# Seven-product mixers: one low half by an adding transfer, inner tiles loaded earlier in the program, weight operands placed by product width

## The chip, the cores and the metric

The kernel runs on one core of one Trainium2 chip. A core has five engines with their own instruction streams: TensorE (PE, matrix products; its weight loads are shown as PEld), VectorE (DVE), ScalarE (ACT), GpSimd (POOL) and SyncE (SP). POOL and SP serve here mainly to issue transfers (DMA). The metric is the device time of one execution in microseconds; lower is better.

## The reference

The model is a two-layer streaming encoder over 512 tokens of width 1024, all in float32. Layer 0 has an RWKV-7 mixer (12 heads of 64) beside a 4-head attention to 256 memory tokens; layer 1 has chunked attention against a shared K/V, again beside memory attention. Each layer ends with the part that the change is about, a convolutional gated mixer:

```python
def conv_glu(h, w_in, conv_w, conv_b, w_out):
    gate, val = jnp.split(h @ w_in, 2, axis=-1)          # 512 x 2816 each
    gp = jnp.pad(gate, ((0, 0), (CONV_W - 1, 0), (0, 0)))
    conv = conv_b + sum(conv_w[j] * gp[:, j:j + seq] for j in range(CONV_W))
    return (jax.nn.gelu(conv, approximate=False) * val) @ w_out
...
x = x + conv_glu(rms_norm(x, ln2[layer]), ffn_in[layer], ffn_conv[layer],
                 ffn_conv_b[layer], ffn_out[layer])
```

`w_in` is 1024 x 5632, that is 22 tiles of 128 gate columns and 22 of 128 value columns. The result must agree with float32 arithmetic, which is why the kernel splits every operand in two.

## The kernel before

**Split operands.** Every dense product runs in TensorE's fp32r format on a high part and a low part of each operand. For one weight tile W and one activation tile X there are three matmuls: Whi·Xhi, Whi·Xlo and Wlo·Xhi. The high part of a weight tile is a rounding copy (ACT). The low part is W - Whi, either a DVE subtraction, or an *adding transfer*: ACT writes -round(W) into the low tile, and then a POOL-issued DMA adds W to it from DRAM.

**Weight buffers.** Pool `wp` holds weight tiles of 128 partitions x 1024 floats (4096 bytes per partition): three for high parts (`whi`), three for low parts (`wlo`), and two (`wraw`) that hold raw weights in most stages and, under the name `wlv`, a low part in the mixers. Activations stand in long-lived tiles of 16384 bytes per partition: `r1h`/`r1l`, `r2h`/`r2l`, `th`/`tl`. Pools lay tiles out in the order of their first use, each rounded up to 32 bytes. In the program before, `r1h` and `r1l` start 32 bytes past a multiple of 128 (`cst` 2840 bytes and `vec` 1264 bytes stand ahead of them), while all `wp` tiles, `r2h`, `r2l`, `th`, `tl` and `sl` start on a multiple of 128.

**Stages.** Up to about 350 us layer 0's RWKV mixer (recurrence work woven with dense projections); to 393 us the output projection; 393 to 713 us the first conv mixer; to 925 us layer 1's attention; to 958 us the output projection; to the end the second conv mixer. In the first conv mixer the activations are U = `r2` and T = `th`/`tl`; in the second U = `r1` and T = `th`/`tl`.

**The input side of a conv mixer** (`ffn`, class `Seven`). 21 of the 22 tiles are done "by seven": the 2 x 2 block product (gate and value block against two halves of the inner dimension, two token halves of 256) takes 7 half-size products in place of 8. One *frame* does one tile j; a product (`prod`, L408) is 4 inner blocks x 3 matmuls of 256 columns, L414 for the two that use a high weight and L416 for the one that uses a low weight. A frame's seven products in order, with their weights and activations: (1) G1 against U, (2) S2 against T, (3) S3 and (4) S1 against T, (5) V2 against T, (6) G2 and (7) S4 against U. G1, V1, G2, V2 are the four raw quarter blocks of 512 columns, S1 to S4 are sums that DVE forms. Each frame also prepares the next tile's weights. The order on DVE and ACT in this stage is the program's (`keep` pins it). What a frame j issues:

- SP: `load` of tile j+1, three transfers (G2 and V2 together, L435; V1 and G1, L437), 1 MB in all, into one of two `raw` buffers. SP carries nothing else in this stage and runs ahead: a transfer goes when its buffer is free, and the last reader of tile j's `raw` is the DVE subtraction of `w4`, in frame j itself.
- ACT: high(G2), a copy of product 1 (L518), high(S4), scale and shift of the gate of tile j-1 (L494, L484), the negative of G2/V2 for the adding transfer (L450), Gelu (L501), high of G1 and S2 of tile j+1, high of its S3 and S1 (all `high`: L468).
- DVE: low of S3/S1 (`lower`, L473), end of tile j-1's gate (L478, L481), low of S4 (`w4`, L473, 512 wide), L535, L498, the sums (L455, L460), L504, L548, low of G1/S2 of tile j+1 (L473, 1024 wide), L464, L561, L563.
- POOL: an adding transfer that finishes the convolution of tile j-1 (L491, 255 KB) and the adding transfer for the low parts of G2/V2 of tile j+1 (`rest`, L451, 512 KB).

**The other places that use `wp` tiles.** `dense` (L221, L222: high weights; L225: low weights) runs 512-column matmuls, weights stationary. `rows` (L658, L663), the output side of a conv mixer (`out_by_seven`), keeps activations stationary and streams a 512-column piece of `whi`/`wlo`. `v_proj` (L1724 to L1726) keeps `r1` stationary and streams 256 columns of a weight tile.

## Time and profile before

| | |
|---|---|
| median of 3 runs | 1302.93 us (1302.65 to 1303.38) |
| the profiled execution | 1301.85 us, of which the span of the profile is 1300.1 us |
| PE busy | 1278.6 us (98%) |
| DVE busy | 1041.8 us (80%) |
| ACT busy | 836.5 us (64%) |
| POOL busy | 137.6 us (11%) |
| transfers | 187.4 MB, 16 DMA engines busy 31.1% for SP's queue and 25.0% for POOL's |

The page gives busy times of each engine, the span in 40 slices, the DMA queues, the chain of work that ended last, and the costliest groups of instructions. PE's busy time is modelled from starts, and consecutive matmuls overlap; how fast PE really goes is read from the distance between the starts of consecutive matmuls in the chain of waits. The timeline gives the start and duration of single instructions on the other engines, and the windows view the busy time of each engine between two moments.

### The profile page before, as it was taken

Reading aid. Unit: us, or ns where it says so; the run is one execution under the profiler, and the core shown is the slowest. Engines: PE = TensorE matmul, PEld = TensorE weight load, DVE = VectorE, ACT = ScalarE, POOL = GpSimd, SP = SyncE. Lnnn points to the kernel's source line nnn. Section 1 sums busy time; section 2 is a strip of 40 time slices with the busy share of each in tenths; the row PEclk is TensorE's granted clock in tenths of the full one; section 3 lists DMA queues with packets and bytes.
Section 4 is the critical chain, followed back from the end, with each engine's and each line's share of the span. In section 5 each row is a group of like instructions: output and inputs, shape, how many; then the busy total and the mean of one; then the engine's idle time right before and its main releaser. Section 6 shows DMA issues by size and latency. Waiting matters only on the chain.

```text
span 1300.1 us, 26329 instructions
## 1 busy us (share of the span) xinstructions
PE 1278.6 (98%) x10420; PEld 1100.9 (85%) x10420; DVE 1041.8 (80%) x1956; ACT 836.5 (64%) x1380; POOL 137.6 (11%) x164
## 2 busy tenths in 40 slices
PE   9999999999999999999999999999999999999997
PEld 7887777777789999999888878787799999998886
DVE  7967767775589999999876876658889999998684
ACT  6666767756566666767554676657757666665562
POOL 1000000000001112110220000000011122111200
PEclk9999999999999999999999999999999999999999
DMA  6365434452236777886984332223437878879951
GB/s 202 110 177 116 112 69 106 95 113 69 82 114 148 182 175 193 189 183 176 270 179 122 123 90 85 81 95 115 130 80 183 183 173 197 186 159 285 214 141 65
DMA packets 92988, 187.42 MB, mean 144 GB/s; under 512 B 21824, under 2 KB 30144, under 8 KB 92864
## 3 DMA queue, kind: packets, MB, share of 16 engines
q1 hardware_dynamic: 68592, 129.14, 31.1%
q0 software_dynamic: 24272, 56.59, 25.0%
q8 instruction: 82, 1.34, 0.4%
q14 instruction: 42, 0.34, 0.1%
HBM read 169.48 MB, written 6.29 MB: 135 GB/s over the span
## 4 chain that ended last, share of the span: by engine, by line
PE 83%; DVE 7%; ACT 6%; issue 1%; DMA 1%; SPq 0%; ACTq 0%; DVEq 0%
PE psf L414 21%; PE psf L416 11%; PE psf L658 7%; PE psd L225 6%; PE psd L221 6%; PE psd L222 5%; PE psf L663 4%; PE psd L658 3%; PE psd L663 2%; PE pss L1774 1%; PE pss L658 1%; DVE wlo L183 1%; PE pss L1404 1%; PE pss L350 1%; PE pss L1760 1%
## 5 line engine op out<-in xcount | busy, mean ns | idle before, releaser
L468 ACT CAST whi<-raw 128x1024 fp32r<-128x1024 f32 (+1 forms) x168 | 151.8, 941 | 66.2 <-PE psf L414 37.4
L414 PE MATMUL psf<-tl,whi 128*128 128x256 f32 x672 | 168.6, 283 | 0.0
L414 PE MATMUL psf<-th,whi 128*128 128x256 f32 x672 | 168.3, 283 | 0.0
L473 DVE TENSOR_TENSOR wlo<-raw,whi 128x1024 fp32r<-128x1024 f32 (+1 forms) x126 | 131.5, 1043 | 14.3 <-ACT whi L468 14.2
L175 ACT CAST whi<-wraw 128x1024 fp32r<-128x1024 f32 x84 | 87.7, 1047 | 69.3 <-PE psd L222 36.1
L414 PEld LDWEIGHTS psf<-tl,whi 128*128 128x128 f32 x672 | 128.7, 192 | 0.0
L414 PEld LDWEIGHTS psf<-th,whi 128*128 128x128 f32 x672 | 128.5, 192 | 0.0
L221 PE MATMUL psd<-r1h,whi 128*128 128x512 f32 x264 | 108.2, 410 | 0.0
L222 PE MATMUL psd<-r1l,whi 128*128 128x512 f32 x264 | 105.6, 401 | 0.0
L183 DVE TENSOR_TENSOR wlo<-wraw,whi 128x1024 fp32r<-128x1024 f32 x65 | 79.3, 1219 | 15.9 <-ACT whi L175 13.6
L648 ACT CAST whi<-raw 128x1024 fp32r<-128x1024 f32 (+1 forms) x52 | 49.6, 954 | 65.2 <-PE psf L658 35.4
L649 DVE TENSOR_TENSOR wlo<-raw,whi 128x1024 fp32r<-128x1024 f32 (+1 forms) x52 | 56.7, 1099 | 42.6 <-ACT whi L648 33.6
L416 PE MATMUL psf<-th,wlo 128*128 128x256 f32 x504 | 81.2, 283 | 0.0
L225 PE MATMUL psd<-r1h,wlo 128*128 128x512 f32 x264 | 74.9, 405 | 0.0
L416 PEld LDWEIGHTS psf<-th,wlo 128*128 128x128 f32 x504 | 69.7, 192 | 0.0
L451 POOL DMA_DIRECT2D wlv<-in_ffn_in_dram x40 | 61.2, 1530 | 59.7 <-DVE tmp L535 58.7
L494 ACT ACTIVATE tmp<-tmp,vec 128x512 f32<-128x512 f32 x44 | 35.9, 817 | 47.3 <-DVE tmp L481 47.1
L414 PE MATMUL psf<-r2h,whi 128*128 128x256 f32 x252 | 63.3, 283 | 0.5 <-ACT whi L468 0.5
L414 PE MATMUL psf<-r2l,whi 128*128 128x256 f32 x252 | 63.2, 283 | 0.0
L414 PE MATMUL psf<-r1h,whi 128*128 128x256 f32 x252 | 62.5, 281 | 0.5 <-ACT whi L468 0.5
L414 PE MATMUL psf<-r1l,whi 128*128 128x256 f32 x252 | 62.1, 279 | 0.0
L221 PEld LDWEIGHTS psd<-r1h,whi 128*128 128x128 f32 x264 | 49.5, 188 | 13.0 <-issue 2.5
(608 smaller groups left out, 3545.7 us busy)
## 6 DMA issues: line engine op xcount, KB each, us to landing
raw<-in_ffn_in_dram SPq DMA_DIRECT2D x42, 512.0 KB, 3.8
raw<-in_ffn_in_dram SPq DMA_DIRECT2D x84, 256.0 KB, 4.2
wlv<-in_ffn_in_dram POOLq DMA_DIRECT2D x40, 512.0 KB, 8.0
raw<-in_ffn_out_dram SPq DMA_DIRECT2D x30, 512.0 KB, 5.9
raw<-in_ffn_out_dram POOLq DMA_DIRECT2D x24, 512.0 KB, 8.0
wraw<-in_wA_dram SPq DMA_DIRECT2D x20, 512.0 KB, 4.2
wraw<-in_w_out_dram SPq DMA_DIRECT2D x16, 512.0 KB, 3.9
wraw<-in_ffn_outp_dram SPq DMA_DIRECT2D x16, 512.0 KB, 4.7
```

The source lines that it names most:

```text
L175: high = lambda: pin(SC.copy(hi[:, :n], raw))
L183: pin(V.tensor_tensor(lo[:, :n], raw, hi[:, :n], op=ALU.subtract))
L221: PE.matmul(ps, wh[:, j * P:(j + 1) * P], ah, start=start and n == 0, stop=False)
L222: dense_at[0] = PE.matmul(ps, wh[:, j * P:(j + 1) * P], al, start=False, stop=False)
L225: dense_at[0] = PE.matmul(ps, wl[:, j * P:(j + 1) * P], act(k)[0], start=False, stop=stop and n == len(ks) - 1)
L414: PE.matmul(ps, wh[:, o + k * P:o + k * P + P], x[k][n], start=k == n == 0, stop=False)
L416: PE.matmul(ps, wl[:, ol + k * P:ol + k * P + P], x[k][0], start=False, stop=k == 3)
L451: GP.dma_start(self.low[:].rearrange("p (a s) -> p a s", a=2), self.second, accum_op=ALU.add)
L468: keep(SC.copy(hi[:, :n], self.pair(what) if n > S else self.raw[:, what]))
L473: keep(V.tensor_tensor(lo[:, :n], self.pair(what) if n > S else self.raw[:, what], hi[:, :n], op=ALU.subtract))
L658: PE.matmul(ps[:], a[:, k0 + i, ts], hi[:, i * S:i * S + S], start=bool(first) and (first is True or t in first) and a is act[0] and i == ...
L663: PE.matmul(ps[:], act[0][:, k0 + i, ts], lo[:, i * S:i * S + S], start=False, stop=bool(last) and t in last and i == n - 1)
```

## The change

1. **Low part of the gate block.** The low part of G1 (first half of `wlo`, 512 columns) is no longer subtracted on DVE together with that of S2. A new step `rest1`, early in frame j, has ACT write -round(G1) of tile j+1 into the first half of the low tile, and POOL issue a 256 KB adding transfer from DRAM onto it. At the place of the old 1024-wide subtraction, `both` takes the high parts as before and subtracts only the 512 columns of S2.
2. **Loads.** `load` of tile j+2 is written in frame j, right behind the subtraction of `w4`, in place of `load` of tile j+1 at the head of frame j; tile 1 is loaded before the frames begin.
3. **Fixed buffers.** `wtile` gives every `whi` and `wlo` tile a named buffer (0, 1, 2 in turn; buffers of the low-rank weights are held until those are done). In the mixers the low part of S3/S1 always takes `wlo` 0, and the low parts of G1/S2 and of S4 of tile j take `wlo` 1 + j mod 2.
4. **Placement.** Every `wp` tile is 1056 floats long (4224 bytes), and the 1024 used start at a chosen float: 16 in the seven-product frames (`W_NARROW`), 0 or 32 everywhere else (`W_AT`, by buffer), 0 for raw tiles. `vec` is 28 floats longer and `rc` 8, which moves the tiles behind them.

```diff
+W_AT = {"whi0": 0, "whi1": 32, "whi2": 0, "wlo0": 32, "wlo1": 0, "wlo2": 32}
+W_NARROW = 16
...
+    turns, held = {"whi": 0, "wlo": 0}, set()
+
+    def wtile(name, dt=F32R, tag=None, at=None, slot=None):
+        if name in turns:
+            n = turns[name] if slot is None else slot
+            while (name, n) in held:
+                n = (n + 1) % 3
+            turns[name] = (n + 1) % 3
+            tag = f"{name}{n}"
+            at = W_AT[tag] if at is None else at
+        else:
+            at = at or 0
+        t = wp.tile([P, 1056], dt, name=name, tag=tag or name, bufs=1 if name in turns else 2)
+        return t[:, at:at + 1024]
...
-    vec = cp.tile([P, NVEC], F32, name="vec")
+    vec = cp.tile([P, NVEC + 28], F32, name="vec")[:, :NVEC]
...
-    rc = cp.tile([P, 4], F32, name="rc")
+    rc = cp.tile([P, 12], F32, name="rc")[:, :4]
...
-        hi = wp.tile([P, 1024], F32R, name="whi", tag="whi")
-        lo = wp.tile([P, 1024], F32R, name="wlo", tag="wlo")
+        hi = wtile("whi")
+        lo = wtile("wlo")
...
             def __init__(self, j):
-                self.j = j
+                self.j, self.slot = j, 1 + j % 2
...
             def rest(self):
-                self.low = wp.tile([P, 1024], F32R, name="wlv", tag="wraw", bufs=2)
+                self.low = wtile("wlv", tag="wraw", at=W_NARROW)
...
+            def rest1(self):
+                self.slot = 1 + self.j % 2
+                self.low1 = wtile("wlo", at=W_NARROW, slot=self.slot)
+                keep(SC.activation(self.low1[:, :S], self.raw[:, G1], AF.Copy, scale=-1.0))
+                GP.dma_start(self.low1[:, :S], A["ffn_in"][l, self.j, 0][:, 0:S], accum_op=ALU.add)
+
+            def both(self):
+                hi = self.high(G1)
+                keep(V.tensor_tensor(self.low1[:, S:2 * S], self.raw[:, S2], hi[:, S:2 * S], op=ALU.subtract))
+                self.gs = hi, self.low1
...
-                hi = wp.tile([P, 1024], F32R, name="whi", tag="whi")
+                hi = wtile("whi", at=W_NARROW)
...
-                lo = wp.tile([P, 1024], F32R, name="wlo", tag="wlo")
+                lo = wtile("wlo", at=W_NARROW, slot={S3: 0, S4: self.slot, G1: self.slot}[what])
...
                 first = prev is None
-                if nxt:
-                    nxt.load()
...
                     hv = self.high(G2)
+                if nxt:
+                    nxt.rest1()
                 keep(SC.copy(g[:, h1], f1[:, h1]))
...
                 w4 = self.lower(S4, self.high(S4, S), S)
+                if self.j + 2 < NFF - 1:
+                    made[self.j + 2].load()
...
                 if nxt:
-                    nxt.gs = nxt.lower(G1, nxt.high(G1))
+                    nxt.both()
                     nxt.sum4()
...
             if m == 1:
                 made[0].load()
+            if m == 5:
+                made[1].load()
...
+        held.update((n_, (turns[n_] + 1 + i_) % 3) for n_ in turns for i_ in range(2))
...
         yield from lora_pair(1, *lw_)
+        held.clear()
...
     run(lora0)
+    held.clear()
```

More of the change, by code (lines that the diff above doesn't have):

```diff
@@ L192, in raw_w @@
     def raw_w(src, n=1024):
-        raw = wp.tile([P, 1024], F32, name="wraw", tag="wraw", bufs=2)
+        raw = wtile("wraw", F32)
         raw_at[0] = nc.sync.dma_start(raw[:, :n], src)
@@ L645, in chunk @@
             else:
-                hi = wp.tile([P, 1024], F32R, name="whi", tag="whi")[:, :n * S]
-                lo = wp.tile([P, 1024], F32R, name="wlo", tag="wlo")[:, :n * S]
+                hi = wtile("whi")[:, :n * S]
+                lo = wtile("wlo")[:, :n * S]
             SC.copy(hi, s_)
@@ L886, in lora_load @@
     def lora_load(idx):
-        raw = wp.tile([P, 1024], F32, name="wraw", tag="wraw", bufs=2)
+        raw = wtile("wraw", F32)
         nc.sync.dma_start(raw[:], A["lora"][idx])
@@ L895, in trunk_kernel @@
     xs += [flat(kt_("AR", (P, NCH, 2, 64), bufs=2), 2) for _ in range(2)]
-    lraw = wp.tile([P, 1024], F32, name="wraw", tag="wraw", bufs=2)
+    lraw = wtile("wraw", F32)
     for m in range(KD):
@@ L902, in trunk_kernel @@
     nc.sync.dma_start(vec[:, 24:], A["vec"][:, 24:])
-    kraw = wp.tile([P, 1024], F32, name="wraw", tag="wraw", bufs=2)
+    kraw = wtile("wraw", F32)
     nc.sync.dma_start(kraw[:], A["wA"][1])
@@ L921, in lora_split @@
     def lora_split(idx, raw, parts=1):
-        hi, lo = zip(*((wp.tile([P, 1024], F32R, name="whi", tag="whi"), wp.tile([P, 1024], F32R, name="wlo", tag="wlo"))
+        hi, lo = zip(*((wtile("whi"), wtile("wlo"))
                        for _ in range(2)))
+        held.update((n_, (turns[n_] + 1 + i_) % 3) for n_ in turns for i_ in range(2))
         mraw = flat(kt_("KB", (P, NCH, 3, 64), bufs=2), 1)[:, 0, 0:1024]
```

## The prediction

> **What bounds the kernel now.** I read the page first (busy times, the chain), then the chain of waits inside a conv mixer, then the windows view and the timeline of one frame. The page, with PE first:
>
> ```profile
> span 1300.1 us, 26329 instructions
> PE 1278.6 (98%) x10420; PEld 1100.9 (85%) x10420; DVE 1041.8 (80%) x1956; ACT 836.5 (64%) x1380; POOL 137.6 (11%) x164
> PE 83%; DVE 7%; ACT 6%; issue 1%; DMA 1%; SPq 0%; ACTq 0%; DVEq 0%
> ```
>
> The chain is 83% PE. In the mixers it is all PE. Here are the chain's rows (start, duration): the first product of two frames that follow each other in the first mixer, then one frame of the second, and one timeline row that names an operand:
>
> ```profile
> 471.53 0.96 PE psf L414 x8
> ...
> 481.61 0.96 PE psf L414 x8
> ...
> 1098.73 0.96 PE psf L414 x8
> ...
> 1103.05 0.95 PE psf L414 x8
> 1104.47 0.94 PE psf L414 x8
> 1105.88 0.94 PE psf L414 x8
> 1107.29 0.95 PE psf L414 x8
> 1108.73 0.96 PE psf L414 x8
> 1103.12 0.28 PE L414 MATMUL psf<-r1h,whi 128*128 128x256 f32 x1
> ```
>
> A product is 12 matmuls. In the first mixer a frame of seven takes 10.08 us (471.53 to 481.61), a product 1.44, a matmul 120 ns. In the second mixer a frame takes 10.00 us: four products at 1.44 us, and the three against `r1`, which start near 1103, in (10.00 - 5.76)/3 = 1.413 us, 117.8 ns a matmul. The form of instruction and the weight buffers are the same; what differs is that `r1` starts 32 bytes past a multiple of 128 while `th`/`tl`, `r2` and the weights stand on one. So the distance of the two operands' addresses has a price, and 512-column matmuls show it with the other sign. These are `dense` blocks (16 + 8 matmuls) at the end of the first mixer (with `r2`) and of the second (with `r1`):
>
> ```profile
> 608.03 0.23 PE psd L221
> 611.66 1.81 PE psd L225 x8
> 613.48 2.72 PE psf L658 x12
> ...
> 1171.48 0.24 PE psd L221
> 1175.21 1.87 PE psd L225 x8
> 1177.08 2.97 PE psf L658 x13
> ```
>
> 5.45 us against 5.60 us for 24: with an offset of 0 a 512-column matmul takes 227 ns, with 32 bytes 233 ns, 6.3 ns more; 256 columns have 2.2 ns less. Nothing else delays PE in a steady frame; how near the others are to being late, from ten frames (PE, PEld, DVE, ACT, POOL, clock, DMA share, GB/s) and one frame's timeline:
>
> ```profile
> 441.29:542.09 100.80, 100.80 (x842) 100.80 (x842) 97.03 (x142) 69.56 (x92) 21.46 (x20) 1.00 0.80 186
> 470.63 1.23 DVE L473 TENSOR_TENSOR wlo<-raw,whi 128x1024 fp32r<-128x1024 f32 x1 [0.31 <-ACT whi L468]
> 473.01 0.37 ACT L518 COPY tmp<-psf 128x256 f32<-128x256 f32 x1 [0.51 <-PE psf L416]
> 474.01 0.62 ACT L468 CAST whi<-raw 128x512 fp32r<-128x512 f32 x1 [0.63 <-PE psf L414]
> 475.77 0.69 DVE L473 TENSOR_TENSOR wlo<-raw,whi 128x512 fp32r<-128x512 f32 x1
> 476.48 0.38 SPq L435 DMA_DIRECT2D raw<-in_ffn_in_dram  x1
> 478.61 1.57 POOL L451 DMA_DIRECT2D wlv<-in_ffn_in_dram  x1
> 480.59 1.23 DVE L473 TENSOR_TENSOR wlo<-raw,whi 128x1024 fp32r<-128x1024 f32 x1 [0.31 <-ACT whi L468]
> ```
>
> DVE is the close second: its own round takes 480.59 - 470.63 = 9.96 us, against PE's 10.08. The granted clock is 1.00.
>
> **The change part by part.**
>
> *Placement, seven-product frames.* `vec` becomes 1376 bytes, so `r1` starts on a multiple of 128 (2848 + 1376 = 33 x 128); weight tiles are 33 x 128 bytes apart, and `W_NARROW` puts weights 64 bytes past. No row shows 256 columns at 64 bytes. Bounds: above, 120 ns, the dearer of the two phases seen; below, half of a good 512-column matmul, 1.81/8/2 = 113 ns. I take 117.8, the `r1` rows: every phase other than 0 that the trace has for 512 columns costs alike, so I read 0 as the special one. First mixer: 21 frames x 7 products x (1.440 - 1.413) = 4.0 us. Second: 21 x 4 x 0.027 = 2.3 us; its `r1` products stay as they are. Together **-6.3 us**, from +0 to (21 x 84 x 7 ns + 21 x (48 x 7 + 36 x 4.8 ns)) = -23 us.
>
> *Placement, 512 columns.* `r1` and the wide weights both stand on multiples of 128, so what takes 233 ns should take 227. How much uses `r1`, by windows of the instructions that touch `r1l`, and, last row, `r1h` (first count: PE):
>
> ```profile
> 30.00:350.00 320.00, 68.91 (x172) 32.17 (x172) 4.74 (x7) 0.00 (x0) 0.00 (x0) 1.00 0.41 98
> 350.00:393.00 43.00, 21.26 (x54) 10.01 (x54) 0.69 (x1) 0.00 (x0) 0.00 (x0) 1.00 0.46 147
> 713.00:925.00 212.00, 46.13 (x144) 27.14 (x144) 7.32 (x14) 0.00 (x0) 0.00 (x0) 1.00 0.31 100
> 1165.00:1177.00 12.00, 6.72 (x18) 3.19 (x17) 0.00 (x0) 0.00 (x0) 0.00 (x0) 1.00 0.68 213
> 1177.00:1300.00 123.00, 29.98 (x126) 23.60 (x126) 6.44 (x6) 5.65 (x6) 0.00 (x0) 0.98 0.65 177
> 1177.00:1300.00 123.00, 30.70 (x127) 23.45 (x126) 6.51 (x6) 5.64 (x6) 0.00 (x0) 0.98 0.65 177
> ```
>
> In `dense` one matmul of three reads `r1l`. Output projection: 3 x 54 x 6.3 ns = 1.0 us; end of the second mixer, 48 x 6.3 = 0.3; its output side, 252 x 6.3 = 1.6; PE bounds all three. Layer 0's mixer has 3 x 172 = 516, up to 3.3 us, but there dense is filler between recurrence work and stands on the chain for a part only:
>
> ```profile
> by line: PE psd L221 9.5%; PE psd L225 8.6%; PE psd L222 8.3%; PE pss L1404 3.1%; issue 3.1%; DMA wraw<-in_w_memv_dram 2.7%; ACT Lc L1174 2.7%; PE pss L1547 2.6%; PE psl L1426 2.2%; PE pss L1259 2.2%; PE pss L1393 2.1%; PE pss L1041 2.0%; P
> 53.04 1.06 ACT whi L175
> ```
>
> 26.4% of 320 us is 84 us, some 360 matmuls, 2.3 us; other work is late right behind it, so I take half, 1.2. Attention: 144 of the 213 us stage are dense (less the 96 of L1725), 48 x 3 x 6.3 = 0.9 us won; but `v_proj` streams 256 columns against `r1`, and its 288 matmuls go from offset 32 to 0, 0.6 us lost; half of the difference, 0.2. Together **-4.3 us**, from -2.9 to -7.1.
>
> *One adding transfer for half a subtraction.* DVE loses 1.23 - 0.69 = 0.54 us a frame; off the path now, yet without it a 9.90 us frame would be under DVE's 9.96. With it DVE's round is 9.42. ACT gains one 512-wide step, 0.62 us, between high(G2) and the copy at 473.01; behind it wait that copy and the cast at 474.01, which had idle times of 0.51 and 0.63, and nothing of PE's waits for the copy until DVE's 476.37 or so. ACT goes from 6.96 to 7.6 us of 9.90. POOL issues one more transfer, ahead of L491 and L451 in its queue: half the size of L451's, so some 0.8 us more of POOL, which is busy 2.1 of 10. The transfer has most of a frame to land. **0**, hidden by PE; without that cover it would cost 0.6 us a frame.
>
> *The new order of buffers.* `w4` of tile j now overwrites the G1/S2 tile that products 1 and 2 read, so on DVE it must wait for product 2, whose end is 471.53 + 2 x 1.44 = 474.41; the row above has it start at 475.77, 0.54 us earlier if DVE gains that. No wait, and behind it on DVE L535 needs product 2 as well. The step `rest1` overwrites the `w4` tile of the frame before, free when that frame ends. **0.** In layer 0 the buffers go in fixed turns; before, a free one was taken. The weight cast at 53.04, on the chain, may then have to wait for a dense product that runs to 55.4: 0 to 2.4 us; I take **+0.5**.
>
> *Loads.* SP issued tile j+2's load at 476.48, the moment `w4` ended (475.77 + 0.69 = 476.46), in frame j already. Writing it there moves nothing. Tile 1's load, written at the head of frame 0 before and ahead of the frames after, also went out long before frame 0 already:
>
> ```profile
> 360.40 0.43 SPq L435 DMA_DIRECT2D raw<-in_ffn_in_dram  x1
> raw<-in_ffn_in_dram SPq DMA_DIRECT2D x20, 256.0 KB, 4.2
> ```
>
> **0.** What `rest1` needs, G1 of `raw`, is the last transfer of a load: out about a microsecond after 476.48, landed 4.2 later near 481.7, and wanted by ACT behind the high(G2) that precedes the next L518 copy, near 482.5. Under 1 us to spare; if it is late, ACT waits, and the copy and the cast behind it have the half microsecond named above.
>
> Sum: -6.3 - 4.3 + 0.5 = -10.1 us. The profiled execution (span 1300.1) took 1301.85 us, 1.1 below the median of 1302.93; so 1291.7 by its own time, about 1292.5 as a median. I forecast **1292**.
>
> A rule of the skill speaks against the largest terms. The Trainium skill ("SBUF — State Buffer", Who interferes with whom) gives PE two independent read ports, for weights and for the moving operand, and says that PE never waits on anyone; by it no placement could matter, and the sum would be +0.5, 1302. The 1.440 and 1.413 us above disagree with it.
>
> **The rivals.**
>
> *Placement does nothing at 64 bytes* (narrow stays at 120 ns, stages woven with other work give nothing): -2.9 + 0.5, **1299.5**; with no effect at all, 1302. For it: the size at 64 is unseen. Against: the two phases seen differ for the same code.
>
> *64 bytes is better than any phase seen.* At 113 ns a frame would be 9.5 us; DVE's 9.42 allows it, the DMA engines (below) just about stop it at 9.66: 21 x 0.42 + 21 x 0.34 = 16 us in place of 6.3, **1282**. The Trainium skill ("TensorE: Matmul & The Clock Gate", Wait — 56ns, not 53.3ns?) has N/2.4 GHz + 2.5 ns, 109 ns for 256 columns; the trace's 227 ns for 512, where it says 216, shows no matmul that fast.
>
> *The phase repeats at 256 bytes, not 128.* By the order of first use, the wide `whi` and `wlo` of buffer 1 stand 128 past a multiple of 256, those of 0 and 2 on one. Then a third of the wide matmuls pay 6.3 ns: a third of the 4.3 is lost, and a third of some 1130 that are good now, 2.4 us: **1296**.
>
> *Slower: the DMA engines become the bound.* Ten frames, and the 40 slices of another 10 us:
>
> ```profile
> q0 software_dynamic: 4279, 8.08, 47.5%
> q1 hardware_dynamic: 5604, 10.49, 32.0%
> wlv<-in_ffn_in_dram POOLq DMA_DIRECT2D x10, 512.0 KB, 7.9
> DMA  8999999989996798999999632100009436999999
> ```
>
> POOL's queue spends 4.79 us a frame on 767 KB; 256 KB more make 1.60, and 0.80 x 10.08 + 1.60 = 9.66 of 9.90 us. If its packets grow 10% longer in the crowd, the engines need 10.6 us and 40 frames x 0.7 us give **1320**; it decides from 9.90, and turns the sign from about 10.15. The first sign would be the L451 transfer: issued at 478.61, landed at 486.5, needed by the low half of product 5 at 481.61 + 4 x 1.44 + 0.96 = 488.3. Against: the slices have over 2 us of idle engines in each frame, between two bursts, just where the new transfer would run, and packets counted in bursts include waiting for each other.
>
> **How the numbers follow.** Forecast 0.50 (own range 1288 to 1297); better phase 0.17; repeat at 256 bytes 0.13; no gain at 64 bytes 0.07, half of it within 0.2% (2.6 us, about what a measurement of this kernel can tell from no change); DMA bound 0.13, one part of it faster or equal. Faster 0.82, same 0.06, slower 0.12. The range takes in the better phase and the unfavourable ends of the terms (0 - 2.9 + 2.4, 1301.4): 1280 to 1301.
>
> **What would show it.** Right: starts of products 1.41 us apart in both mixers, also against `th`; `dense` blocks with `r1` at 1.81; DVE near 93% in a frame; L435 still at the end of `w4`. Wrong: gaps between products (a frame longer than 84 matmuls), PE waiting for `wlv` or `wlo` behind a DMA, a mixed 1.81/1.87 in `dense`, or layer 0's mixer ending later than 350 us.

## The result: slower, and where the time is

The changed kernel takes 1312.28 us (median of 6 runs, 1309.39 to 1314.53), the kernel before 1303.16 us beside it; the ratio is 1.0071, with a 95% interval of 1.006 to 1.0082. The forecast was 1292 us, in a range of 1280 to 1301: it is missed by 20 us, and on the wrong side.

The profiled execution of the changed kernel took 1309.39 us. Its page (span; busy times by engine; the chain by engine):

```profile
span 1307.6 us, 26473 instructions
PE 1267.3 (97%) x10420; PEld 1085.2 (83%) x10420; DVE 1022.2 (78%) x1956; ACT 858.1 (66%) x1420; POOL 172.3 (13%) x204
PE 75%; DVE 7%; ACT 7%; DMA 7%; issue 3%; SPq 0%; ACTq 0%; DVEq 0%
```

PE is busy 11 us less than before, in a span that is 7.5 us longer. Its share of the chain fell from 83% to 75%, and the share of the transfers rose from 1% to 7%. So the placement made the matmuls faster, and PE now waits for something that comes out of a transfer.

Here is the chain of waits of the changed kernel in one such place, the start of a frame in the first mixer (start, duration; line numbers are 19 to 30 higher than before: L433 and L435 are the old L414 and L416, L548 the old L518, L475 the new copy in `rest1`, and L498 the old L468):

```profile
499.45 7.40 DMA raw<-in_ffn_in_dram
...
506.95 0.04 ACT wlo L475
...
507.48 0.36 ACT tmp L548
...
507.89 1.20 PE psf L433 x8
509.09 0.45 PE psf L435 x4
509.54 0.91 PE psf L433 x8
510.45 0.45 PE psf L435 x4
510.90 0.91 PE psf L433 x8
```

Read it from the bottom. Products follow each other at 510.90 - 509.54 = 1.36 us (1.44 before). The one at 507.89 is product 3: it waited for ACT's copy of product 1 (L548). ACT was late with that copy because it executes in order, and ahead of the copy stood `rest1`'s copy of G1 (L475), which waited until G1 of the raw block had landed, 7.4 us after its issue.

How often this happens, by the waits of the changed kernel between 410 and 590 us, 18 frames (in total, times, longest), and the transfers of 100 us (450 to 550; KB each, median us to landing):

```profile
ACT wlo L475 <- DMA raw<-in_ffn_in_dram: 17.5, 15, 2.0
PEld psf L433 <- ACT tmp L548: 5.6, 9, 1.1
PE psf L433 <- ACT tmp L548: 3.9, 8, 0.9
raw<-in_ffn_in_dram SPq DMA_DIRECT2D x22, 256.0 KB, 6.2
wlv<-in_ffn_in_dram POOLq DMA_DIRECT2D x10, 512.0 KB, 9.4
```

In 15 of 18 frames ACT waits for G1, and in about half of them PE waits for ACT. The 256 KB transfers of a load took 4.2 us before and take 6.2 now. Frames come in two kinds: unhindered ones of 9.52 us (10.08 before), and others of 9.65 to 10.8.

To see all stages together, I compared when the k-th matmul of PE's stream starts in each trace. The table has the length of each segment before, and the difference to it of the changed kernel and of three kernels from the experiments below (e2: placement alone, corrected; e11: the changed kernel with another order of the load; e13: with three corrections).

| segment (k of its ends), us | before | changed | e2 | e11 | e13 |
|---|---|---|---|---|---|
| layer 0's RWKV mixer (to 4200) | 324.92 | +0.37 | +2.13 | +0.79 | -0.32 |
| output projection (to 4500) | 59.73 | -0.60 | -1.04 | -0.60 | -1.01 |
| into the first mixer, first frame (to 4650) | 20.72 | +4.21 | +2.85 | +2.63 | -0.06 |
| frames of the first mixer (to 6240) | 190.80 | -3.55 | -2.81 | -9.97 | -9.72 |
| its end (to 6450) | 42.08 | +1.87 | +1.23 | +2.25 | +1.22 |
| output side, layer 1's attention (to 8100) | 317.28 | +0.61 | -0.23 | +0.71 | -0.33 |
| first frames of the second mixer (to 8250) | 18.94 | +1.58 | -0.12 | +1.37 | -0.16 |
| frames of the second mixer (to 9700) | 172.90 | +2.24 | -0.97 | -8.24 | -7.88 |
| its end (to 9900) | 29.09 | +1.55 | +1.27 | +2.71 | +0.53 |
| its output side (to 10350) | 100.50 | -0.80 | -1.54 | -0.81 | -1.56 |

The "changed" column adds up to +7.5 us, the difference of the two spans; the profiled execution of the changed kernel is the fastest of its six, so the medians are further apart, 9.1 us. Two things stand out: the frames, where some 18 us were to be had (e11) and little over 1 arrived, and the 4.2 us on the way into the first mixer (2.6 of them stay in e11).

Part of the second comes from PE's clock. In some traces PE was granted half its clock for stretches of 3.41 us; here are two such places in the windows view (PE, PEld, DVE, ACT, POOL, clock, DMA share, GB/s), the changed kernel's first frame and e2's layer 0:

```profile
394.97:401.80 6.83, 5.95 (x28) 5.95 (x29) 5.41 (x13) 3.10 (x5) 2.07 (x2) 0.50 0.45 111
49.34:52.75 3.41, 3.41 (x17) 3.41 (x17) 3.41 (x23) 1.43 (x3) 0.00 (x0) 0.50 0.51 159
```

At such a clock the narrow matmuls start 213 ns apart in place of 113.5 (e2, near 398 us), so a stretch costs PE up to 1.7 us. The changed kernel's trace has two of them, one behind the other, on the way into the first mixer, e2's one there and one near 49 us, e11's one each near 396, 956 and 1161 us. The traces of before and of e13 have none ahead of the last microseconds. What sets them off isn't shown: e7 and e13 both have a pause of PE of 1.02 us near 393 us, and only e7 has the halved clock behind it.

Where the matmuls stand alone, the trace also shows what the placement did to 512-column matmuls. These are low-half blocks (8 matmuls each) of the changed kernel's last output side, from the chain:

```profile
1185.35 3.73 PE psf L690 x16
1189.07 1.87 PE psf L695 x8
1190.94 3.64 PE psf L690 x16
1194.58 1.81 PE psf L695 x8
1196.39 3.63 PE psf L690 x16
1200.02 1.81 PE psf L695 x8
```

1.87, 1.81, 1.81: one buffer in three is at the slow distance. Before, the three rows that answer to these were at 1.81 or 1.82.

### The profile page after: what moved, and what is told of

Same layout as the page of the kernel before. It is cut to its first block, busy times and chain, and to the rows that moved or that the text cites. A ratio compares the mean times of both kernels' runs of the same rounds, so it can differ in the third digit from the quotient of the medians.

```text
span 1307.6 us, 26473 instructions
## 1 busy us (share of the span) xinstructions
PE 1267.3 (97%) x10420; PEld 1085.2 (83%) x10420; DVE 1022.2 (78%) x1956; ACT 858.1 (66%) x1420; POOL 172.3 (13%) x204
## 4 chain that ended last, share of the span: by engine, by line
PE 75%; DVE 7%; ACT 7%; DMA 7%; issue 3%; SPq 0%; ACTq 0%; DVEq 0%
PE psf L433 16%; PE psf L690 7%; PE psf L435 7%; PE psd L244 6%; PE psd L240 5%; PE psd L241 5%; PE psf L695 4%; DMA raw<-in_ffn_in_dram 3%; PE psd L690 3%; DMA wraw<-in_ffn_in_dram 2%; PE psd L695 2%; PE pss L1811 1%; PE pss L690 1%; DVE wlo L202 1%; PE pss L1439 1%
## 5 line engine op out<-in xcount | busy, mean ns | idle before, releaser
L498 ACT CAST whi<-raw 128x1024 fp32r<-128x1024 f32 (+1 forms) x168 | 157.4, 943 | 63.5 <-DVE raw L490 32.6
L433 PE MATMUL psf<-th,whi 128*128 128x256 f32 x672 | 165.9, 283 | 15.5 <-ACT tmp L548 12.7
L433 PE MATMUL psf<-tl,whi 128*128 128x256 f32 x672 | 163.1, 279 | 0.0
L433 PEld LDWEIGHTS psf<-th,whi 128*128 128x128 f32 x672 | 127.3, 190 | 20.6 <-ACT tmp L548 17.1
L433 PEld LDWEIGHTS psf<-tl,whi 128*128 128x128 f32 x672 | 127.6, 190 | 0.0
L503 DVE TENSOR_TENSOR wlo<-raw,whi 128x1024 fp32r<-128x1024 f32 (+1 forms) x86 | 82.7, 962 | 20.3 <-ACT whi L498 19.9
L680 ACT CAST whi<-raw 128x1024 fp32r<-128x1024 f32 (+1 forms) x52 | 49.5, 952 | 61.3 <-PE psf L690 32.1
L681 DVE TENSOR_TENSOR wlo<-raw,whi 128x1024 fp32r<-128x1024 f32 (+1 forms) x52 | 56.6, 1099 | 39.8 <-ACT whi L680 32.0
L435 PE MATMUL psf<-th,wlo 128*128 128x256 f32 x504 | 79.0, 278 | 0.0
L476 POOL DMA_DIRECT2D wlo<-in_ffn_in_dram x40 | 36.3, 908 | 249.1 <-ACT tmp L548 245.4
L435 PEld LDWEIGHTS psf<-th,wlo 128*128 128x128 f32 x504 | 67.6, 190 | 0.0
L433 PE MATMUL psf<-r2h,whi 128*128 128x256 f32 x252 | 60.4, 276 | 0.0
L433 PE MATMUL psf<-r1h,whi 128*128 128x256 f32 x252 | 60.4, 276 | 0.0
L433 PE MATMUL psf<-r1l,whi 128*128 128x256 f32 x252 | 60.4, 276 | 0.0
L433 PE MATMUL psf<-r2l,whi 128*128 128x256 f32 x252 | 60.4, 276 | 0.0
```

The lines of the kernel that those rows point to most:

```text
L433: PE.matmul(ps, wh[:, o + k * P:o + k * P + P], x[k][n], start=k == n == 0, stop=False)
L435: PE.matmul(ps, wl[:, ol + k * P:ol + k * P + P], x[k][0], start=False, stop=k == 3)
L498: keep(SC.copy(hi[:, :n], self.pair(what) if n > S else self.raw[:, what]))
L503: keep(V.tensor_tensor(lo[:, :n], self.pair(what) if n > S else self.raw[:, what], hi[:, :n], op=ALU.subtract))
```

## The experiments

Theory at the start: **transfers**. The adding transfer, or what it does to the loads, costs what the placement wins. Rivals: **placement** (the new distances are no gain, or one of them is a loss) and **buffers** (the fixed turns make somebody wait). A single frame has three limits, and the first runs take them apart: PE's 84 matmuls, DVE's round, and the transfers.

### Placement alone (e1), and with the wide operands at 0 of 256 bytes (e2)

e1 is the changed kernel without `rest1`/`both` and with the loads back in their old place:

```diff
-                if nxt:
-                    nxt.rest1()
...
-                    nxt.both()
+                    nxt.gs = nxt.lower(G1, nxt.high(G1))
...
-                if self.j + 2 < NFF - 1:
-                    made[self.j + 2].load()
```

> Placement and fixed buffers alone: the low part of G1 is subtracted on DVE again (1024 wide) and the loads stand where they stood before. Theory 'transfers' (the new adding transfer fills the DMA engines, the raw loads land late, the new ACT step waits for them at the head of a frame and holds the copy behind it that PE needs): no gaps between products; DVE is the bound with its round of 9.96 us, so 21 x 0.12 + 21 x 0.05 = 3.6 us less than before, and about 1 us from the wide products, 1298 to 1300 us. Rival 'buffers' (the fixed turns of the buffers make PE wait): gaps stay, over 1305. Rival 'placement' (the new addresses slow something): over 1305 with longer single instructions.

e2 moves the two odd buffers of the wide matmuls in addition:

```diff
-W_AT = {"whi0": 0, "whi1": 32, "whi2": 0, "wlo0": 32, "wlo1": 0, "wlo2": 32}
+W_AT = {"whi0": 0, "whi1": 0, "whi2": 0, "wlo0": 32, "wlo1": 32, "wlo2": 32}
```

> As e1_place_only, with the start of two buffers changed (whi1 at float 0, wlo1 at float 32) so that all wide weights stand on a multiple of 256 bytes. If the phase of 512-column matmuls repeats at 256 bytes, the 631 that ran at 232.6 ns against a buffer 128 bytes off go to 227: some 3 us less than e1_place_only, 1295 to 1297 us. If it repeats at 128: no difference to e1_place_only.

Measured: e1 1304.73 us (ratio 1.0013, 1.0004 to 1.0023), e2 1301.73 us (0.9995, 0.9986 to 1.0004). The difference of 3.0 us is that of a distance which repeats at 256 bytes and not at 128. In e2's output side all low-half blocks are at 1.81.

But e1 was expected some 5 us lower. Its frames are 9.96 us, not 9.52, with a third of a microsecond of idle PE in nearly each. One wait of e1 and two timeline rows of e2, one frame apart, show the limit (410 to 590 us; then start, duration, engine):

```profile
PEld psf L435 <- DVE wlo L503: 3.8, 15, 0.3
```

```profile
473.65 1.23 DVE L503 TENSOR_TENSOR wlo<-raw,whi 128x1024 fp32r<-128x1024 f32 x1 [0.31 <-ACT whi L498]
483.62 1.23 DVE L503 TENSOR_TENSOR wlo<-raw,whi 128x1024 fp32r<-128x1024 f32 x1 [0.31 <-ACT whi L498]
```

DVE's round is 9.97 us, as in the kernel before, and PE's 84 matmuls now take less. Placement alone can't use more than 0.1 us a frame: it needs the relief of DVE that the adding transfer was to give.

### The transfer without the placement (e3), and everything but the transfer (e4)

e3 is the changed kernel with 1024-float tiles, `W_AT` and `W_NARROW` all 0, and `vec` and `rc` as before. e4 is the changed kernel without one line:

```diff
-                GP.dma_start(self.low1[:, :S], A["ffn_in"][l, self.j, 0][:, 0:S], accum_op=ALU.add)
```

> The adding transfer, the earlier loads and the fixed buffers without the placement: tiles of 1024 floats, all starts at 0, vec and rc as before. Theory 'transfers': PE's frame is 10.08 us again, and the DMA engines, 9.7 us a frame, just keep up, but the first frames (+6 us in the first mixer, +3 in the second) and the two ends of the mixers (+2 each) keep their loss: 1311 to 1317 us. Rival 'placement': 1302 to 1304, since nothing else costs. Rival 'buffers': over 1305 too.

> The changed kernel without the adding transfer of rest1; ACT still writes the 512 columns, so the low part of G1 is wrong, and only its time is read. Theory 'transfers': raw loads land in about 4 us again, no gaps between products, frames of 9.52 us (84 x 113.4 ns): 42 x 0.52 = 22 us less than before, 1280 to 1285 us. Rival 'buffers': the gaps stay, about 1310.

Measured: e3 1319.54 us (1.0128, 1.011 to 1.0146); e4 1291.50 us (0.9912, 0.9891 to 0.9933). Both are some us above what was expected (e3 has two first frames of 15.4 and 17.2 us, and e4 loses 2.5 us on the way into the first mixer like e1), but the side is clear. In e4 nearly all frames are at 9.52 us, with DVE relieved, ACT still making the copy, and the DMA share at 0.84 in place of 0.98. So in the changed kernel the one transfer of 256 KB costs 1312.3 - 1291.5 = 20.8 us, give or take some 3 us by the intervals. Its two simplest readings stay: the DMA engines are full, or something is late.

### Relieving DVE by GpSimd in place of the transfer (e5)

e2 with the 512-wide sum for S4 on GpSimd inside the mixers:

```diff
-                keep(V.tensor_tensor(raw[:, S4], raw[:, S2], raw[:, G2], op=ALU.add))
+                keep((GP if pinned[0] else V).tensor_tensor(raw[:, S4], raw[:, S2], raw[:, G2], op=ALU.add))
```

> The kernel of e2 (placement alone, all wide operands at 0 of 256 B), but the add of S4 (the 512-wide add of 0.68 us a frame on DVE) goes to GpSimd inside the mixers. Theory 'DVE's round': in e2 the frame stood at 9.96 us because DVE has 9.96 us of work in it while PE has 9.52; with one add less DVE has some 9.3 and PE sets the frame: 9.52 us, 0.44 us less in each of about 38 frames, so some 17 us less than e2's 1301.7, 1283 to 1288. Rival: what holds e2's frames is not DVE's sum of work but one late operation, or GpSimd's own queue (it issues the adding transfer and the copies of the residual there) makes the sum late: frames stay at 9.9 or grow, 1301 or more.

Measured: 1310.36 us (1.0055, 1.004 to 1.007), frames of 10.14 us: the theory's number was missed by more than 20 us. Timeline of e5 (POOL, then DVE in the same frame):

```profile
453.41 2.02 POOL L494 TENSOR_TENSOR raw<-raw 128x512 f32<-128x512 f32 x1
```

```profile
454.52 2.00 DVE L503 TENSOR_TENSOR wlo<-raw,whi 128x1024 fp32r<-128x1024 f32 x1 [0.31 <-ACT whi L498]
457.38 1.21 DVE L503 TENSOR_TENSOR wlo<-raw,whi 128x1024 fp32r<-128x1024 f32 x1
```

The sum takes 2.0 us on GpSimd (0.68 on DVE), and the DVE subtraction that runs beside it takes 2.00 us in place of 1.21. DVE saves 0.60 us (from the sum's start to the next instruction's, 454.87 to 455.48 in e2) and loses 0.79: its round goes from 9.96 to some 10.14, and that is the frame. The limit was DVE's sum of work, as the theory had it; the relief was none. The Trainium skill ("SBUF — State Buffer", Who interferes with whom) says that a DVE instruction with two SBUF inputs contends with a GpSimd instruction that reads SBUF; these two rows agree with it.

### ACT's order (e6): the copy of G1 behind the copy of product 1

```diff
-                if nxt:
-                    nxt.rest1()
                 keep(SC.copy(g[:, h1], f1[:, h1]))
+                if nxt:
+                    nxt.rest1()
```

> The changed kernel with one move: ACT's negative copy of G1 and the adding transfer behind it come after ACT's copy of product 1 instead of ahead of it. Theory 'ACT's order': the new gaps (PE's third product waits for that copy, which stands on ACT behind the cast that waits for the raw block) go; mixer frames of 9.86 and 10.04 us fall to about 9.6, so 10 to 17 us less than the changed kernel's 1312: 1295 to 1302. Rival 'DMA engines': the transfers fill the 16 engines (share near 1.0), so what is late stays late and only the instruction that shows it changes: PE then waits for the low block of G1 or for a cast; 1309 to 1314.

Measured: 1308.07 us (1.0029, 1.0006 to 1.0052; runs from 1301.59 to 1310.03): 4 us less than the changed kernel. The theory's 1295 to 1302 is missed; the rival's 1309 to 1314 is nearly met, and the trace shows what it named: what is late stays late and another instruction shows it. PE no longer waits for the copy of product 1. But ACT waits for G1 just as long (group of e6: 19 copies, busy, mean, idle before them), and what stands behind it in ACT's order is late instead, as is the next transfer (waits of e6):

```profile
L475 ACT ACTIVATE wlo<-raw 128x512 fp32r<-128x512 f32 x19 | 12.0, 633 | 19.3 <-DMA raw<-in_ffn_in_dram 19.3
```

```profile
PEld psf L435 <- DMA wlv<-in_ffn_in_dram: 6.1, 10, 1.3
```

So one place further back in ACT's order isn't enough (a place still further back wasn't tried); the moment at which G1 is there has to change.

### G1 as the first transfer of the load (e11)

A load is three transfers. In the changed kernel, as before, G1 is the last of them, and `rest1` is the first that wants anything of it.

```diff
-                nc.sync.dma_start(self.raw[:, G2:V2 + 1], self.second)
-                for o, a in ((V1, 1), (G1, 0)):
+                for o, a in ((G1, 0), (V1, 1)):
                     nc.sync.dma_start(self.raw[:, o], A["ffn_in"][l, self.j, a][:, 0:S])
+                nc.sync.dma_start(self.raw[:, G2:V2 + 1], self.second)
```

> The changed kernel with G1's transfer as the first of a tile's load instead of the last. Theory 'ACT's order': ACT's copy at the head of the frame no longer waits for it, the copy of product 1 behind it is on time, and the waits of PE's third product for that copy go, as in e6: 1302 to 1308. Rival 'DMA engines': the other two transfers of the load land as late as G1's did, the sums of the next tile and the casts behind them are late instead: 1309 to 1316.

Measured: 1291.79 us (0.9911, 0.9897 to 0.9926), 20.5 us less than the changed kernel and better than the theory had asked. The transfers are all there, and within the intervals it is as fast as e4, which leaves the adding one out. The group of `rest1`'s copy between 410 and 590 us, first the changed kernel, then e11 (count, busy, mean; idle time before them):

```profile
L475 ACT ACTIVATE wlo<-raw 128x512 fp32r<-128x512 f32 x18 | 11.4, 633 | 20.0 <-DMA raw<-in_ffn_in_dram 17.5 <-PE psf L433 1.6 <-PE psf L435 0.7
```

```profile
L475 ACT ACTIVATE wlo<-raw 128x512 fp32r<-128x512 f32 x18 | 11.3, 626 | 0.0
```

And the windows of 100 us in the changed kernel, e4 and e11 (PE, PEld, DVE, ACT, POOL, clock, DMA share, GB/s):

```profile
450.00:550.00 100.00, 98.05 (x854) 97.18 (x853) 92.24 (x142) 75.33 (x103) 30.22 (x31) 1.00 0.98 213
```

```profile
450.00:550.00 100.00, 100.00 (x885) 100.00 (x884) 95.50 (x147) 79.09 (x107) 21.45 (x20) 1.00 0.84 194
```

```profile
450.00:550.00 100.00, 100.00 (x885) 100.00 (x884) 95.64 (x148) 79.14 (x106) 30.94 (x31) 1.00 1.01 222
```

e11 has a DMA share of 1.01, more than the changed kernel, and PE does as many matmuls in the window (885) as without the transfer. **By this share the DMA engines are full, and they are not the bound; that G1 lands last is what cost the 20 us.** With the same bytes in the same queues and G1 first, ACT doesn't wait for G1 in any of the 18 frames; PE waits for `wlv` once, for 0.5 us.

### A plain transfer in place of the adding one (e10), and one in every second frame (e9)

```diff
-                GP.dma_start(self.low1[:, :S], A["ffn_in"][l, self.j, 0][:, 0:S], accum_op=ALU.add)
+                GP.dma_start(self.low1[:, :S], A["ffn_in"][l, self.j, 0][:, 0:S])
```

> The changed kernel with the transfer of the gate block's low part as a plain one of the same bytes from the same place, without adding (the low part of G1 is then wrong: the block itself and not the block less its high part). In the trace a packet of 2 KB takes 178 ns when it adds and 84 ns when it doesn't. Theory 'packet time': the price of the transfer is the DMA engines' time; the plain one takes half, the mixers' DMA share falls from 0.98 to about 0.9, and most of the 20.8 us between the changed kernel and e4 goes: 1292 to 1300. Rival 'one more transfer': what costs is its issue on GpSimd's queue and its wait, whatever its packets: 1308 to 1313.

e9 also has the edits of e2 and, further down, of e7, and its `rest1` stands behind the copy of product 1 as in e6:

```diff
-                if nxt:
+                keep(SC.copy(g[:, h1], f1[:, h1]))
+                if nxt and nxt.j % 2:
                     nxt.rest1()
-                keep(SC.copy(g[:, h1], f1[:, h1]))
...
-                    nxt.both()
+                    if nxt.j % 2:
+                        nxt.both()
+                    else:
+                        nxt.gs = nxt.lower(G1, nxt.high(G1))
```

> The changed kernel with three corrections: wide operands all at 0 of 256 B (e2), the buffer turn of e7, and the adding transfer of the gate block's low part only for every second tile, put behind ACT's copy of product 1 (e6); the other tiles take it on DVE as before. Theory 'DMA engines and DVE share the frame': with a transfer in each frame the DMA share is near 1.0 and frames are late, without one DVE's 9.96 us sets them; with one in two frames DVE has some 9.7 us a frame on the mean and the DMA share is some 0.9, so mean frames near 9.7 and a time of 1290 to 1294, below both kernels. Rival: one adding transfer more is one too many wherever it falls (frames of 10.2 to 10.7 after each), 1300 or more.

Measured: e10 1293.78 us (0.9933, 0.9915 to 0.9951), e9 1292.90 us (0.9919, 0.9904 to 0.9934). Both numbers came as expected, but e11 shows that their theory names the wrong part. With less traffic G1 lands earlier (256 KB in 5.6 us in e10, against 6.2), and ACT's wait for it falls from 17.5 to 7.3 us in 18 frames. It is the same lateness made smaller; the bytes themselves have room. e9 changes four things at once, so what its missing transfers alone are worth can't be read from it. By themselves the two runs would pass for proof that the DMA engines are the bound.

### The loads alone (e12)

e2 with tile j+2's load behind `w4`, as in the changed kernel.

> The kernel of e2 (placement alone) with the loads of a tile given out one frame earlier as in the changed kernel, and no other transfer. Both theories on the transfer expect nothing from the earlier loads by themselves: the raw block is there long before its first reader either way, DVE's 9.96 us sets the frame: 1300 to 1303. Rival 'earlier loads do the harm' (they run beside the adding transfer of the other half and delay it): 1305 or more.

Measured: 1301.78 us (0.9989, 0.998 to 0.9999), e2's time. The earlier place of the loads in the program does nothing by itself.

### The buffer turns (e7, e8)

In the table e2 still loses 2.85 us on the way into the first mixer. DVE writes the low part of the output projection's last weight there; kernel before, then e2, then PE's matmuls that read it in e2:

```profile
378.03 1.22 DVE L183 TENSOR_TENSOR wlo<-wraw,whi 128x1024 fp32r<-128x1024 f32 x1
```

```profile
387.46 1.22 DVE L202 TENSOR_TENSOR wlo<-wraw,whi 128x1024 fp32r<-128x1024 f32 x1
388.74 2.11 PE L244 MATMUL psd<-r1h,wlo 128*128 128x512 f32 x8
```

By the addresses, this low part has `wlo` buffer 2 in e2, which the product before it reads until 383.7; the buffer whose readers ended at 372.8 is passed over, because tile 0's G1/S2 takes buffer 1 and moves the turn on. The eight matmuls then come after product 1, and the norm that the rest of the frame needs comes after them: 16.9 us for this frame, 11.9 before. e7 leaves the turn where it was:

```diff
+                turn = turns["wlo"]
                 lo = wtile("wlo", at=W_NARROW, slot={S3: 0, S4: self.slot, G1: self.slot}[what])
+                if self.j == 0 and what == G1 and turn != self.slot:
+                    turns["wlo"] = turn
```

> The kernel of e2 with the turn of the low buffers not moved on when the first tile takes its own: the low part of the last weight of layer 0's output projection then gets the buffer that has long been read, not the one that the product before is still reading. Theory 'buffer turns': in e2 that low part is written 9 us later than in the kernel before (387.5 against 378.0) and the first frame of the first mixer is 16.9 us long against 11.9; with the other buffer the frame is 12 us again: 5 us less than e2's 1301.7, near 1296.7. Rival: the first frame is late for another reason (order of the queue, casts): 1301 to 1302.

e8 takes e1 back to rotating pools of three, without turns and held buffers; the wide low parts then start at float 32 of whichever buffer they get, and the wide high parts at float 0:

```diff
-            n = turns[name] if slot is None else slot
...
+        at = (32 if name == "wlo" else 0) if at is None else at
+        t = wp.tile([P, 1056], dt, name=name, tag=tag or name, bufs=3 if name in turns else 2)
```

> The kernel of e1 (placement alone), but the high and low tiles come from rotating pools of three as in the kernel before instead of fixed buffers with turns; tiles of 1056 columns, narrow at 64 B, wide at 0 or 128 of 256 B as the pool's turn falls. Theory 'buffer turns': the losses of e1 against the kernel before outside the frames (3.1 us at the start, 4.4 us in the first mixer's first frame) go, and the frames stay at DVE's 9.96: 1295 to 1298. Rival: the fixed buffers cost nothing, and what e1 lost is due to the phases or the order: 1303 to 1306.

Measured: e7 1299.78 us (0.9975, 0.9964 to 0.9985), 1.9 less than e2 where 5 were expected; e8 1301.33 us (0.9988, 0.9979 to 0.9998), 3.4 less than e1 where 7 or more were. In both the low part is written in time again, begun by 378.4 at the latest, and the first frame of the first mixer falls to 13.8 us (e7) and 11.9 (e8). So the buffer turn is the cause of the late low part, but the sizes were misjudged. In e2 product 1 runs ahead of the eight late matmuls, so the length of the frame overstates what they cost: e7's frame is 3.1 us shorter and begins 1.8 us later within its segment, which wins 1.3 us.

The rest goes with the halved clock. e7 wins another 1.3 us in layer 0's mixer, where e2's trace has a stretch of it near 49 us and e7's none; and it loses 1.4 us to e2 in the second mixer's first frames, where e7 has one (958.95 to 962.36) and e2 none. Both have one in the first mixer's first frame, and e8 has none: that is most of the 1.9 us between their first frames. e8 wins 2.9 us in the segment and 2.0 in layer 0 against e1, which has a halved stretch in each, and gives back 1.6 in the frames, which are no shorter than DVE's 9.96 us.

### All three corrections (e13), and the order of the load without the placement (e14)

e13 is the changed kernel with the edits of e11, e2 and e7. e14 is e3 with the edit of e11.

> The changed kernel with three corrections that were measured apart: G1 first in the load (e11, 20.5 us less than the changed kernel), wide operands all at 0 of 256 B (e2, 3.0 us less than e1), the buffer turn of the first tile (e7, 1.9 us less than e2). Theory 'three separate losses': they stand at different places of the span, so they add: e11's 1291.8 less 5, 1287 (1285 to 1289), frames of 9.52 us throughout. Rival 'the same wait': no less than e11, 1290 to 1293.

> The kernel of e3 (transfer, earlier loads and fixed buffers without the placement, 1319.5 us) with G1 first in the load. Theory 'order of the load': the waits of PE for the copy of product 1 go here too and the frames fall to PE's 10.08 us, what stays is the first frame's loss and the start: 1305 to 1311. Rival: without the placement G1's place is not what cost; the time stays at 1317 or more. By both the kernel before is not beaten, since PE's 10.08 us sets the frame there as well.

Measured: e13 1283.83 us (0.9852, 0.9837 to 0.9866), 28.5 us below the changed kernel and faster than both. e14 1308.59 us (1.0039, 1.0024 to 1.0053), 11 less than e3, with every frame after the second at 10.08 us in the first mixer and 10.00 in the second. The order of the load removes the waits there as well, and what then sets the frame is PE at the old distances. e13's page, and its chain through one frame of the first mixer:

```profile
span 1280.7 us, 26475 instructions
PE 1255.1 (98%) x10420; PEld 1081.0 (84%) x10420; DVE 1021.4 (80%) x1956; ACT 861.5 (67%) x1420; POOL 172.0 (13%) x204
```

```profile
500.00 0.91 PE psf L433 x8
500.90 0.45 PE psf L435 x4
...
509.51 0.91 PE psf L433 x8
```

Seven products in 9.51 us, and PE is the bound again. e13 is 3 us better than expected: against e11 it wins 8.0 us where the parts had given 3.0 + 1.9. By the table (10 us between the two profiled executions) it wins at the start of both mixers (2.7 and 1.5 us), at their ends (1.0 and 2.2), and about 1 us each in layer 0, layer 1's attention and the last output side. e11's three stretches of halved clock, up to 5.1 us, stand at three of these places (both starts and the second end), and e13's trace has none. Over the whole span e11's runs were granted 0.994 to 0.997 of the clock and e13's 0.997 to 0.998, so this is not the profiled executions alone; whether the corrections bring it about or chance does, wasn't tried.

## Why the prediction was wrong, point by point

**The step that failed is the last of the part on the change: "Loads", taken at 0.** It found the right place. G1 is the last transfer of a load, wanted near 482.5 and landed near 481.7, "under 1 us to spare". But the landing of 4.2 us came from the trace of before, with a DMA share of 0.80, and was used for a kernel whose share the same text put at 9.66 of 9.90. Measured, the landing is 6.2 us (7.4 in the frame shown). And the cover of "half a microsecond" behind it was smaller than the lateness: ACT's waits go up to 2.0 us, and PE's third product stands behind the copy. The tight margin should have had a price, or a rival of its own. e11 measures it: 20.5 us between the medians, and 16.9 us in the frames of the two traces.

**The adding transfer, taken at 0.** Right, once its input is in time: e11 and e4 differ by 0.3 us, within their intervals. As the change has it, 20.8 us. ACT's additional 0.62 us and POOL's additional issue are indeed hidden.

**The slower rival, "the DMA engines become the bound".** It had the right sign and nearly the time (1320 against 1312), for a wrong reason: that it came near is luck. Its first sign, PE waiting for the `wlv` transfer, didn't come: `wlv` lands later (9.4 us against 7.9), but the waits of the changed kernel's first mixer have no PE wait for it. The 9.66 us that it took for a floor is none; e11's frames are at 9.52.

**Placement of the narrow matmuls, -6.3 us.** Right in sign, too small. At 64 bytes a 256-column matmul starts every 113.5 ns, not every 117.8: the reading that distance 0 is the special case and all others are alike fell. That was the rival "64 bytes is better than any phase seen", with 113 ns and 16 us. With nothing in the way (e13) the frames win 9.7 + 7.9 = 17.6 us. That e11, the change with one order corrected, lands on the forecast 1292 is luck too: its frames win 18.2 us, and 9.0 are lost at the starts and ends of the mixers, for which the forecast had nothing.

**Placement of the wide matmuls, -4.3 us.** With all operands at 0 of 256 bytes (e2), the output projection wins 1.04 us (forecast 1.0), the last output side 1.54 (1.6), the stage with the attention 0.23 (0.2). Layer 0's mixer shows little of its 1.2: in e13, with the same places and no halved clock there, it is 0.3 us shorter. That the filler there is covered by other work would fit, but wasn't tried. As the change places them, the rival "repeats at 256 bytes" holds (631 matmuls at the slow distance), and the gains are about half: 0.60 and 0.80. e2 against e1 puts this at 3.0 us; the rival had 3.8.

**The new order of buffers, +0.5.** The price was looked for at the weight cast near 53 us and lies at 378: the low part of the output projection's last weight. "In layer 0 the buffers go in fixed turns" was followed to the one cast that stood on the chain, and not to the last tile before the mixer, where tile 0 takes a buffer out of turn. The way into the first mixer is 2.6 us longer for it in e11, where G1 is in time, with up to 1.7 of these under a halved clock, and not at all in e13.

**The two favourable rivals and the unfavourable one were treated as exclusive.** Better phase, repeat at 256 bytes and a late transfer hold at once, and the lateness kept the gain of the first from arriving. The chances were dealt out as if one of them had to be true alone.

**What stays open.** The ends of the mixers are 0.5 to 2.7 us longer in all kernels of the table with the shorter frames. PE waits there for the adding transfer that fills the last low part (0.7 to 2.0 us by the waits of these traces; its matmuls waited for none before); an earlier issue wasn't tried. In layer 0's mixer the halved clock near 49 us goes with e2's +2.13 us (e1 and e12 have it too, +2.25 and +1.94). What sets the halved clock off, and the rest of the differences there (-0.3 to +0.8 us in the table), I didn't find.

## What to carry to other kernels

Before a step is given a new first reader, look which transfer of its input lands last and put that reader's first; the same bytes in the same queues were worth 20 us of 1312 in another order. Don't take a landing time from a trace with idle transfer engines for a kernel that fills them; a margin under a microsecond in front of an in-order engine is a term of the sum, not a remark. And a run that removes traffic and gets faster doesn't show that bandwidth is the bound: change the order at full traffic before you say so.

## What the runs showed of the hardware

**The distance between the operands' addresses.** I took the time from each matmul's start to the next, and the start address of its moving operand less that of the following weight block, modulo 256 bytes. 256 columns: 119.9 ns at 0 and 117.8 at 32 (before), 113.5 to 113.6 at 64 and 192 (some 3400 matmuls, changed kernel). 512 columns: 227 (median) at 0 and 233 at 32 (before), and 232.6 at 128 (631 matmuls, changed kernel). So the narrow and the wide form want different distances: the wide one is fast at 0 and not at 128 of 256 bytes, and the narrow one is slow at 0, where the wide one is fast. The rule of the Trainium skill that the prediction cited ("SBUF — State Buffer", Who interferes with whom), that PE's ports never wait, gives no room for 113.5 against 120; why the distance matters, no run here shows.

**Adding packets.** The 2 KB packets of the adding transfers take 178 ns in the median, those of the plain loads 84 ns (changed kernel, 450 to 550 us). It is the adding and not the queue: the plain transfer that e10 issues from POOL in its place takes 99 ns a packet.

**A share of 1.0.** e11 holds a DMA share of 1.01 over 100 us in which PE starts as many matmuls (885) as with a share of 0.84 (e4), and e13 a share of 1.00 with 880, though the 512 KB part of a load then lands after 6.6 to 6.7 us in place of 3.8. A full share says how late a transfer will be, not yet who waits for it.

**GpSimd beside DVE.** An elementwise add on GpSimd (2.0 us for 512 columns) made the DVE subtraction beside it 0.79 us longer.

**The granted clock.** In stretches of 3.41 us PE was granted 0.50 of its clock: one or more ahead of the program's last microseconds in most traces, none in those of before, e8 and e13. Each is worth up to 1.7 us, as much as the smaller effects of this document, so single traces are compared segment by segment with the clock beside them.
